# The second half of the input projection by seven products for eight: a decoder trunk on one core

## The chip, the core and the metric

The kernel runs on one core of a Trainium2 chip. A core has a matrix engine (TensorE, PE in the profile; its weight loads are PEld), a vector engine (VectorE, DVE), a scalar engine for functions (ScalarE, ACT), a general engine (GpSimd, POOL) and SyncE (SP), which here only issues transfers. Data lie in device memory (HBM), in SBUF (128 partitions), or in PSUM, where TensorE writes its sums: eight banks of 128 x 512 float32. The metric is the device time of one execution in microseconds (us); the median of several runs is compared.

## The reference

One decoder layer on x of 2048 positions x 1024 channels, float32:

```python
z = rms_norm(x, g1) @ w_in                       # 1024 -> 3584
lru_x, lru_gate, sc_b, sc_c, sc_x = split(z)     # 1024, 1024, 512, 512, 512
lru_x = causal_conv4(lru_x) + bias
y_lru = rg_lru(lru_x) * gelu(lru_gate)           # 16 heads of 64, gates r and i, a scan over positions
y_sc  = sc_b * causal_conv3(sc_c * sc_x)
x = x + concat(y_lru, y_sc) @ w_out              # 1536 -> 1024
h = rms_norm(x, g2)
gate, up = split(causal_conv3(h @ w_up))         # 1024 -> 6144
x = x + (gelu(gate) * up) @ w_down               # 3072 -> 1024
out = rms_norm(x, gf)
```

In the RG-LRU, r and i are sigmoids of 64 x 64 products per head, a = exp(-8 r softplus(-lambda)), and h[t] = a[t] h[t-1] + sqrt(1 - a[t]^2) i[t] x[t].

## The kernel before

Channels lie on the partitions, positions along the free dimension. The positions are worked in two halves of T = 1024, each of two blocks of NB = 512 (a PSUM bank holds 128 channels x 512 positions). Every operand of a product is split into two parts (`split`, L197 to L199: ScalarE makes the rounded part, VectorE the rest), and each product is three matmuls: high x high, high x low, low x high.

The order on TensorE, SyncE and GpSimd is the order in which the program is written (`manual_schedule`). ScalarE and VectorE are ordered by a planner, by priority: earlier in the program comes first, and `high_priority` moves an instruction ahead (HP = 120 for what empties PSUM, HW = 90 for weights of plain products). That order is fixed when the program is built. SyncE issues transfers one after the other; a transfer whose source is not ready holds the ones behind it. `defer(n, ...)` puts a store on a list and `tick()` (called with each load of weights) counts it down and issues what is due.

The stages, in order: input projection of half 0 (`in_phase(0)`), output product of half 0 (`sweeps(0)`), input projection of half 1 (`in_phase(1)`), output product of half 1, up product of half 0, down product of half 0, up and down product of half 1.

The input projection is a plain product: 28 output blocks of 128 channels (`in_product`), each 8 chunks of 128 input channels x 3 x 2 blocks of positions = 48 matmuls, into two banks. The result is multiplied by the inverse root of the mean square while it leaves PSUM (`evac`). Blocks 0 to 7 are lru_x, 8 to 15 lru_gate, 16 to 19 sc_b, 20 to 23 sc_c and 24 to 27 sc_x. They are consumed by units in the order UNITS: L0 to L7 are the LRU blocks (`lru_conv`, `lru_gates`, `lru_scan`), S0 to S3 the gated convolutions (`sc_first`, `sc_second`). Two units together give the operands of the output product (`combine_even`, `combine_odd`), which are stored to device memory (y_d) and read again by the sweeps.

The output, up and down products already use a scheme of seven products of half-size blocks in place of eight (in the manner of Strassen and Winograd): `sweeps` for output and down, with the sums of weights made in device memory by transfers that add (`sums`, `sum_step`), and `Pair` for the up product, with the sums of weights made on VectorE (`up_weights`) and the seven operands B11, B21, B22, T1 to T4 of the other side made by `h_prep`. A Pair makes two output blocks at once with 7 x 4 chunks x 3 = 84 matmuls. One bank collects W11 B11, then S2 T2, S3 T3 and W22 T4, and is copied out after each; two more banks take S1 T1 + S4 B22 and W12 B21, which are added on VectorE.

Pages in SBUF are taken from pools: "act" of 28 pages of 128 x 1024, "w" of 10 (split weights), "tmp" of 7, "wr" of 4 raw pages of 128 x 1536, and four longer pages for what needs a halo. An instruction that needs a page waits until the earlier owner is done with it.

The x of half 1 is prepared beside the output product of half 0 (`x1_beside`, `x_prep`), unnormalised.

## Time and profile before

| what | us |
|---|---|
| runs shown: 2275.12, 2275.98, 2272.85; median | 2275.12 |
| profiled execution, span from first to last instruction | 2273.5 |
| TensorE busy in it | 2254.4 (99%) |
| VectorE busy | 1721.1 (76%) |
| ScalarE busy | 1178.9 (52%) |
| GpSimd busy | 138.2 (6%) |
| input projection of half 0, from 5.7 | 323.6 |
| output product of half 0, from 329.3 | 114.2 |
| input projection of half 1, from 443.5 | 325.3 |
| output product of half 1, from 768.8 | 116.4 |

Of the profiled execution the span is the time that its trace gives; the time beside it, the median, is that of other executions, timed without a trace. The stages are read from the chain of waits, where TensorE changes from one product's tile to the next (zin_b: input projection; ox and oy: output; zx, za, zc: up; dx and dy: down). A matmul's duration in the profile overlaps that of its neighbours, so a count of matmuls is turned into time by the distance of their starts. "Idle before, <- releaser" names what an instruction waited for.

### The profile page before, as it was taken

How to read it: one execution, taken by the hardware profiler on the slowest of the kernel's cores; microseconds unless marked ns; L12 is line 12 of the kernel's file. 1: busy time of each engine (PE TensorE's matmuls, PEld its weight loads, DVE VectorE, ACT ScalarE, POOL GpSimd, SP SyncE). 2: the span in 40 equal slices, each digit the busy share in tenths (PEclk: the TensorE clock that was granted, in tenths of full speed). 3: DMA queues.
4: the chain of work that ended last, by engine and by line, in shares of the span. 5: the costliest groups of instructions: out<-in, count | busy, mean ns of one | idle time of the engine just before them, and what ended most of it. 6: DMA issues, size and time to landing. Idle time of an engine off the chain costs nothing.

```text
span 2273.5 us, 26241 instructions
## 1 busy us (share of the span) xinstructions
PE 2254.4 (99%) x9982; PEld 1855.7 (82%) x9982; DVE 1721.1 (76%) x1956; ACT 1178.9 (52%) x1311; POOL 138.2 (6%) x188
## 2 busy tenths in 40 slices
PE   9999999999999999999999999999999999999997
PEld 7888888888887888888888888888888888888886
DVE  8765678758757898888888887587888888886556
ACT  6674745564668255544444444454544444443343
POOL 0100000010000000111111100000100000000000
PEclk9999999999999999999999999999999999999999
DMA  8642258768644586233232357676223232358755
GB/s 275 141 139 74 70 175 297 274 166 217 195 123 136 199 282 204 92 107 107 98 111 95 113 190 263 207 250 201 70 105 114 92 117 88 118 183 319 259 194 176
DMA packets 146446, 377.24 MB, mean 166 GB/s; under 512 B 14160, under 2 KB 17872, under 8 KB 145744
## 3 DMA queue, kind: packets, MB, share of 16 engines
q1 hardware_dynamic: 136384, 356.69, 45.5%
q0 software_dynamic: 9792, 18.88, 5.1%
q8 instruction: 78, 1.28, 0.2%
q14 instruction: 48, 0.39, 0.0%
q10 hardware_dynamic: 144, 0.00, 0.0%
HBM read 288.48 MB, written 124.78 MB: 182 GB/s over the span
## 4 chain that ended last, share of the span: by engine, by line
PE 91%; ACT 4%; DVE 3%; issue 1%; DMA 0%; DVEq 0%; SPq 0%; ACTq 0%
PE zx L632 23%; PE zin_b L241 20%; PE dx L752 11%; PE zc L632 11%; PE dy L752 9%; PE za L632 6%; PE ox L752 6%; PE oy L752 4%; DVE cv L302 1%; ACT r L343 1%; ACT i L343 1%; PE zr_b L333 0%; ACT L343 0%; DVE r L356 0%; DVE wl_in L199 0%
## 5 line engine op out<-in xcount | busy, mean ns | idle before, releaser
L241 PE MATMUL zin_b<-xh,wh_in 128*128 128x512 f32 x896 | 280.2, 394 | 3.8 <-ACT i L343 3.3
L241 PE MATMUL zin_b<-xl,wh_in 128*128 128x512 f32 x896 | 277.1, 390 | 0.0
L241 PE MATMUL zin_b<-xh,wl_in 128*128 128x512 f32 x896 | 276.8, 390 | 0.0
L241 PEld LDWEIGHTS zin_b<-xh,wh_in 128*128 128x128 f32 x896 | 167.8, 189 | 45.2 <-ACT i L343 4.4
L241 PEld LDWEIGHTS zin_b<-xl,wh_in 128*128 128x128 f32 x896 | 169.1, 189 | 35.5 <-DVE xl L418 0.3
L241 PEld LDWEIGHTS zin_b<-xh,wl_in 128*128 128x128 f32 x896 | 168.8, 188 | 35.3
L199 DVE TENSOR_TENSOR fl_d<-wrf_d,fh_d 128x1024 fp32r<-128x1024 f32 x84 | 102.8, 1223 | 120.9 <-ACT fh_d L198 118.5
L198 ACT ACTIVATE fh_d<-wrf_d 128x1024 fp32r<-128x1024 f32 x84 | 89.0, 1060 | 202.5 <-PE dy L752 83.4
L199 DVE TENSOR_TENSOR wla_up<-wra_up,wha_up 128x1024 fp32r<-128x1024 f32 x48 | 58.8, 1226 | 141.6 <-ACT wha_up L198 141.6
L752 PE MATMUL dx<-fh_d,wh_d 128*128 128x512 f32 x384 | 149.4, 389 | 0.0
L752 PE MATMUL dx<-fl_d,wh_d 128*128 128x512 f32 x384 | 149.4, 389 | 0.0
L752 PE MATMUL dx<-fh_d,wl_d 128*128 128x512 f32 x384 | 149.4, 389 | 0.0
L632 PE MATMUL zc<-hhB,whd_up 128*128 128x512 f32 x384 | 126.0, 389 | 0.0
L302 DVE SCALAR_TENSOR_TENSOR cu<-un,prm,cu 128x1024 f32<-128x1024 f32 x96 | 122.6, 1277 | 4.3 <-ACT cu L298 4.3
L302 DVE SCALAR_TENSOR_TENSOR cg<-ug,prm,cg 128x1024 f32<-128x1024 f32 x96 | 122.8, 1279 | 0.4
L643 ACT ACTIVATE ug<-zx 128x512 f32<-128x512 f32 x96 | 57.6, 600 | 126.1 <-PE zx L632 126.1
L632 PE MATMUL zx<-ht,whc_up 128*128 128x512 f32 x384 | 118.2, 389 | 0.0
L752 PE MATMUL dy<-fh_d,wh_d 128*128 128x512 f32 x288 | 112.0, 389 | 0.0
L752 PE MATMUL dy<-fl_d,wh_d 128*128 128x512 f32 x288 | 112.0, 389 | 0.0
L752 PE MATMUL dy<-fh_d,wl_d 128*128 128x512 f32 x288 | 112.0, 389 | 0.0
L199 DVE TENSOR_TENSOR wl_d<-wrw_d,wh_d 128x1024 fp32r<-128x1024 f32 x84 | 102.4, 1219 | 12.3 <-ACT wh_d L198 10.9
L199 DVE TENSOR_TENSOR wl_in<-wr_in,wh_in 128x1024 fp32r<-128x1024 f32 x53 | 64.6, 1219 | 58.1 <-ACT wh_in L198 58.1
(267 smaller groups left out, 5576.1 us busy)
## 6 DMA issues: line engine op xcount, KB each, us to landing
wr_in<-in_w_in SPq DMA_DIRECT2D x53, 512.0 KB, 5.7
wra_up<-in_w_up SPq DMA_DIRECT2D x48, 512.0 KB, 4.6
wrb_up<-in_w_up SPq DMA_DIRECT2D x48, 512.0 KB, 5.1
f_d_T<-cg SPq DMA_DIRECT2D x96, 256.0 KB, 2.5
wrw_d<-sd_d_S SPq DMA_DIRECT2D x48, 512.0 KB, 4.6
wrf_d<-f_d_T SPq DMA_DIRECT2D x48, 512.0 KB, 3.9
f_d_B<-cu SPq DMA_DIRECT2D x72, 256.0 KB, 2.4
wrw_d<-in_w_down SPq DMA_DIRECT2D x36, 512.0 KB, 4.7
```

Source lines behind the costliest of these rows:

```text
L198: nc.scalar.activation(r32(hi), src, AF.Copy)
L199: nc.vector.tensor_tensor(r32(lo), src, hi, ALU.subtract)
L241: nc.tensor.matmul(ps[t], r32(a), r32(b[:, blk(t)]), start=(first and i == 0), stop=(last and i == 2))
L302: nc.vector.scalar_tensor_tensor(dst, src[:, k : k + T], col(o_w + k), dst, ALU.mult, ALU.add)
L343: nc.scalar.activation(dst[rows, blk(b)], p[HALVES[at], :], AF.Sigmoid, bias=col(o + c)[rows, :])
L632: nc.tensor.matmul(ps, r32(p[:, s]), r32(self.hs[k][x][o]), start=f and i == 0, stop=l and i == 2, skip_group_check=True,)
L643: nc.scalar.activation(dst, self.x, AF.Copy)
L752: nc.tensor.matmul(ps[m], r32(p), r32(x[:, k, :]), start=first and i == 0 and n == 0, stop=(last or not on_x) and i == ni - 1 and n == 2, ...
```

## The change

The second half's input projection now uses the scheme of seven products too.

- The first half, which loads and splits every block of w_in anyway, adds two blocks' halves on VectorE in place (`pair_sums`, three additions of 128 x 512 for each pair of blocks) and stores the sums (si_d). It also stores the split gate weights (sg_d).
- The order of units becomes L0 L1 S0 S1 L2 to L7 S2 S3, with the two gated convolutions of a pair done together.
- Beside the first half's units the x of half 1 is read, squared and summed, its mean taken, and the first of four groups of operands made (`beside_first`, `x1_prep`, which shares `operands` with `h_prep`; the norm is now applied before the products). The other three follow beside the sweeps of half 0, at steps 3, 8 and 14.
- The second half runs `in_blocks`: 14 pairs in the order PAIRS, L for lru_x and lru_gate, X for sc_c and sc_x, B for two blocks of sc_b. Each pair's seven weights are split into seven pages (`in_weights`). An LRU block's gates and scan are worked during the next pair. Its r and i take pages of "tmp", the stored gate weights of four blocks are loaded into a "tmp" page at the first block of the four.
- The first pair of this stage and of each up product runs chunk by chunk: seven banks at once, each chunk of input channels through all seven products (`spread`).
- The inverse norm of half 0's output is stored (ms_d) and read back in the next sweeps. The four preparations of the up product of half 0 all move beside the sweeps of half 1 (steps 1, 6, 11, 16; before, one in the projection, and three at steps 3, 8, 14).
- The pool "w" of ten is cut into "w" and "v" of five each, which plain products use in turn.

```diff
-UNITS = [(u[0], int(u[1])) for u in "L0 L1 S0 L2 L3 S1 L4 L5 L6 L7 S2 S3".split()]
+UNITS = [(u[0], int(u[1])) for u in "L0 L1 S0 S1 L2 L3 L4 L5 L6 L7 S2 S3".split()]
+PAIRS = [(u[0], int(u[1])) for u in "L0 L1 X0 X1 B0 L2 L3 L4 L5 L6 X2 L7 X3 B2".split()]
...
+BLOCKS = {
+    **{("L", c): (c, 8 + c) for c in range(8)},
+    **{("X", g): (20 + g, 24 + g) for g in range(4)},
+    **{("B", g): (16 + g, 17 + g) for g in range(0, 4, 2)},
+}
+PAIR_OF = {o: (PAIRS.index(p), i) for p, ab in BLOCKS.items() for i, o in enumerate(ab)}
+
+TERMS = [("W11", "B11"), ("S2", "T2"), ("S3", "T3"), ("W22", "T4"), ("S1", "T1"), ("S4", "B22"), ("W12", "B21")]
...
+        return page(name, "wv"[turn[0] % 2], 5)
...
+    def load_weights(o, name, gate=None):
         tick()
+        raw_of[o] = raw_tile(f"wr_{name}")
+        out = next(load_parts(w_in[o], name, 1, gate, raw_of[o]))
+        i, _ = PAIR_OF[o]
+        pair_sums(*BLOCKS[PAIRS[i]])
         return out
+
+    def pair_sums(a, b):
+        if a not in raw_of or b not in raw_of:
+            return
+        i, _ = PAIR_OF[a]
+        ra, rb = raw_of.pop(a), raw_of.pop(b)
+        with tc.high_priority(offset=HW):
+            for t, k, x, y in (
+                (rb, 2, rb[:, 0, :], rb[:, 1, :]),
+                (rb, 0, rb[:, 0, :], ra[:, 0, :]),
+                (ra, 0, ra[:, 0, :], rb[:, 2, :]),
+            ):
+                nc.vector.tensor_tensor(t[:, k, :], x, y, ALU.add)
+        defer(2, si_d[i][:, 0:2, :], rb[:, 0:3:2, :])
+        defer(2, si_d[i][:, 2, :], ra[:, 0, :])
...
+        defer(1, sg_d[c // 4, :, c % 4, :], gw[:, : 2 * P])
...
+        r, i = (flat((home or act)(f"{x}{n}")) for x in "ri")
+        a = big(f"a{n}", c % 2)[:, :T] if home else flat(act(f"a{n}"))
...
+    def keep_y(half, n, y, when):
+        if n % 2 == 0:
+            yc = flat(tmp(f"yc{half}_{n}"))
+            even_y[n // 2] = (y, yc)
+            combine_even(y_d[half], when[0], n // 2, y, yc)
         else:
-            pss = [in_product(o, half, acts) for o in (0, NLRU)]
+            even, yc = even_y.pop(n // 2)
+            combine_odd(y_d[half], when[1], n // 2, even, y, yc, flat(tmp(f"yd{half}_{n}")))
...
+            keep_y(half, n, y, (2, 8) if n >= NOUT - 2 else (7, 7))
...
+        def spread(self):
+            self.open()
+            ps = {w: pst(f"z{w}{self.name}") for w, _ in TERMS}
+            for k in range(4):
+                for w, x in TERMS:
+                    self.run(ps[w], w, x, True, True, (k,))
+            (g0, g1), (n0, n1) = self.g, self.n
+            self.x = ps["W11"]
+            self.copy(g0)
+            with tc.high_priority(offset=HP):
+                for dst, w, src in (
+                    (g1, "S2", g0),
+                    (n1, "S3", g1),
+                    (n0, "W22", n1),
+                    (n1, "S1", n1),
+                    (g1, "S1", g1),
+                    (g1, "S4", g1),
+                    (g0, "W12", g0),
+                ):
+                    nc.vector.tensor_tensor(dst, ps[w], src, ALU.add)
+            self.second_done()
+            self.first_done()
...
+            if j == 0:
+                cur.spread()
+                nxt.begin()
+                nxt.sum1()
...
+    def in_weights(i):
+        a, b = BLOCKS[PAIRS[i]]
+        one, other = raw_tile(f"wra_in{i}"), raw_tile(f"wrb_in{i}")
+        nc.sync.dma_start(one[:, 0, :], w_in[a][:, :NB])
+        nc.sync.dma_start(one[:, 1:3, :], si_d[i][:, 1:3, :])
+        nc.sync.dma_start(other[:, 0, :], w_in[a][:, NB:])
+        nc.sync.dma_start(other[:, 1, :], w_in[b][:, NB:])
+        nc.sync.dma_start(other[:, 2, :], si_d[i][:, 0, :])
+        tick()
+        out = {}
+
+        def operand(name, src):
+            w = page(f"w{name}_in{i}", "v" if i == 0 and name in ("W22", "S4") else "w", 5)
+            split(w[:, 0, :], w[:, 1, :], src)
+            out[name] = (w[:, 0, :], w[:, 1, :])
+
+        operand("W11", one[:, 0, :])
+        operand("S1", one[:, 1, :])
+        operand("S2", one[:, 2, :])
+        nc.vector.tensor_tensor(one[:, 2, :], one[:, 2, :], other[:, 0, :], ALU.add)
+        operand("W12", other[:, 0, :])
+        operand("S3", other[:, 2, :])
+        operand("W22", other[:, 1, :])
+        operand("S4", one[:, 2, :])
+        return out
...
+        def load_gates(q):
+            t = tmp(f"gp{q}")
+            state["gw"] = flat(t).rearrange("p (c k) -> p c k", c=NLRU // 2)
+            nc.sync.dma_start(state["gw"], sg_d[q])
+
+        def finish(pair):
+            n = UNITS.index(("L" if pair.kind == "L" else "S", pair.unit))
+            if pair.kind == "L":
+                c = pair.unit
+                xc, cv = lru_conv_of(c, half, pair.first, vpage)
+
+                def gated():
+                    if c % 4 == 0:
+                        load_gates(c // 4)
+                    g = state["gw"][:, c % 4, :]
+                    return lru_gates(c, half, xc, (g[:, :P], g[:, P:]))
+
+                def scanned(pss):
+                    y = lru_scan(c, half, cv, pair.other, *pss, home=tmp, sign=-1.0)
+                    keep_y(half, n, y, (1, 1))
+
+                gates[pair.name] = (gated, scanned)
+            elif pair.kind == "X":
+                pr, cc = pair.first[:, 2 : 2 + T], pair.other
+                nc.vector.scalar_tensor_tensor(pr, pr, -1.0, cc, ALU.mult, ALU.mult)
+                cv = flat(vpage(f"sv{pair.name}"))
+                conv(cv, pair.first, 3, O_SCW + 3 * pair.unit)
+                sv[pair.unit] = cv
+            else:
+                for i, b in enumerate((pair.first, pair.other)):
+                    cv = sv.pop(pair.unit + i)
+                    for t in range(T // NB):
+                        h = blk(t)
+                        nc.vector.scalar_tensor_tensor(cv[:, h], cv[:, h], -1.0 if i else 1.0, b[:, h], ALU.mult, ALU.mult)
+                    keep_y(half, n + i, cv, (1, 1))
...
+        cur = InPair(0, hs, wts[0])
+        last = None
+        for j in range(len(PAIRS)):
+            if j + 2 < len(PAIRS):
+                wts.append(in_weights(j + 2))
+            else:
+                tick()
+            nxt = InPair(j + 1, hs, wts[j + 1]) if j + 1 < len(PAIRS) else None
+            if j == 0:
...
+                cur.spread()
+                nxt.begin()
...
+            if last is not None:
+                gated, scanned = gates.pop(last)
+                pss = gated()
+                scanned(pss)
+                last = None
+            if nxt is not None and j + 2 < len(PAIRS):
+                nxt.sum1()
+            if j > 0:
+                cur.end()
+            finish(cur)
+            if cur.name in gates:
+                last = cur.name
+            start(j)
...
+    def beside_first(n):
+        if n == 0:
+            ss1[1] = acc_tile("a1")
+        if 1 <= n <= KC:
+            t = x1_raw.pop(n - 1)
+            if n == 1:
+                nc.scalar.activation(ss1[1], t, AF.Square)
+            else:
+                nc.scalar.activation(t, t, AF.Square)
+                nc.vector.tensor_tensor(ss1[1], ss1[1], t, ALU.add)
+        if n < KC:
+            t = x1_raw[n] = flat(act(f"xs{n}"))
+            nc.sync.dma_start(t, xT[n, :, T:S])
+        if n == KC:
+            x1_raw["mean"] = mean_split(ss1[1], "a1")
+        if n == KC + 1:
+            inv_rms(ss1[1], "a1", x1_raw["mean"])
+        if n == KC + 2:
+            hx.append(x1_prep(0, ss1[1]))
...
+        if s in (3, 8, 14):
+            hx.append(x1_prep(len(hx), ss1[1]))
...
+    def beside_blocks(j):
+        if j == 0:
+            inv_rms(ss2[0], "b0", mean0)
+            defer(1, ms_d, ss2[0])
+        sum_step()
+        sum_step()
+
+    in_blocks(hx, beside_blocks)
...
+    prepare = h_beside(0, (1, 6, 11, 16))
+
+    def out1_beside(s):
+        if s == 0:
+            t = acc_tile("b0r")
+            nc.sync.dma_start(t, ms_d)
+            rs2[0].append(t)
+        prepare(s)
...
```

276 lines of the change are left out of this document (154 added, 122 removed).

## The prediction

> **What bounds the kernel now.** I read first the page, for who is busy; then the chain of waits, for which engine carries the end; then windows over the stages the change touches; then single rows for prices.
>
> ```profile
> span 2273.5 us, 26241 instructions
> PE 2254.4 (99%) x9982; PEld 1855.7 (82%) x9982; DVE 1721.1 (76%) x1956; ACT 1178.9 (52%) x1311; POOL 138.2 (6%) x188
> ...
> L241 PE MATMUL zin_b<-xh,wh_in 128*128 128x512 f32 x896 | 280.2, 394 | 3.8 <-ACT i L343 3.3
> ```
>
> TensorE is busy 2254.4 of 2273.5 us, so what shortens the kernel is fewer matmuls, and what lengthens it is a new gap in front of one. The 394 ns of a row here are not the price of a matmul, since they overlap. The chain of waits (start, length, what) has the price and the borders of the stages:
>
> ```profile
> 54.14 11.10 PE zin_b L241 x48
> ...
> 443.53 21.76 PE zin_b L241 x96
> ...
> 768.83 15.65 PE ox L752 x69
> ...
> 803.59 16.32 PE ox L752 x72
> ```
>
> 96 matmuls took 21.76 us: 0.2267 us each. The second half's input projection runs from 443.53 to 768.83, and the first two sweeps of the output product behind it end at 803.59: 360.1 us for both. The stages' windows (length, then busy us of PE, PEld, DVE, ACT, POOL):
>
> ```profile
> 5.70:329.30 323.60, 322.74 (x1445) 262.20 (x1446) 224.57 (x288) 203.57 (x227) 11.95 (x13) 1.00 0.48 148
> 329.30:443.50 114.20, 114.20 (x505) 94.59 (x505) 97.25 (x108) 62.76 (x63) 0.00 (x0) 1.00 0.73 256
> 443.50:768.80 325.30, 322.81 (x1450) 262.45 (x1449) 217.00 (x233) 195.08 (x210) 21.66 (x25) 0.99 0.63 178
> 768.80:885.20 116.40, 114.88 (x506) 94.51 (x505) 106.16 (x120) 57.03 (x59) 0.34 (x4) 1.00 0.74 253
> ```
>
> In the projection of the second half VectorE works 217 and ScalarE 195 of 325.3 us, two thirds and 60%; in the sweeps behind it VectorE already works 106 of 116.4.
>
> **The gross gain.** 28 products of 48 matmuls (1344) become 14 pairs of 84 (1176). 168 x 0.2267 = 38.1 us. In full, the new stage without any gap is 1176 x 0.2267 = 266.6, eight gate products at 1.66 (the first gate row below, at 52.48, to the projection's row at 54.14) = 13.3, one mean of four matmuls 0.9, and the two sweeps 2 x 16.32 = 32.6: 313.4 us. Against 360.1 that is 46.7 less, so it also wins back 8.6 us that the stage loses now. The mean of the second half's x moves into the first half (0.9 us of PE), which leaves 45.8.
>
> ```profile
> 52.48 0.49 PE L333 MATMUL zr_b<-xch,gw 64*128 64x512 f32 x1
> ...
> 661.05 0.49 PE L333 MATMUL zr_b<-xch,gw 64*128 64x512 f32 x1
> ...
> 684.62 0.49 PE L333 MATMUL zr_b<-xch,gw 64*128 64x512 f32 x1
> ...
> 722.53 0.50 PE L241 MATMUL zin_b<-xh,wh_in 128*128 128x512 f32 x1 [1.58 <-ACT i L343]
> 723.93 0.79 PE L241 MATMUL zin_b<-xh,wh_in 128*128 128x512 f32 x1 [0.90 <-ACT i L343]
> ```
>
> The last two rows are part of those 8.6 us: TensorE waits 1.58 and 0.90 us for sigmoids to empty banks. What follows them (length, busy us, clock):
>
> ```profile
> 722.00:724.00 2.00, 0.57 (x2) 0.84 0.00 0
> 724.00:726.00 2.00, 2.00 (x5) 0.50 0.00 0
> 726.00:728.00 2.00, 2.00 (x9) 0.81 0.81 272
> ```
>
> The granted clock falls to 0.50 and costs 2 x (0.16 + 0.50 + 0.19) = 1.7 us more. I add 1.7 us to each new gap that is longer than this one. The Trainium skill ("TensorE: Matmul & The Clock Gate", Part 1) says that throttling needs an idle window of about 3.4 us; here 2.5 us were enough, and the measurement decides. By the Trainium skill the shortest of the gaps below would go without the surcharge, 1.7 us less in the sum.
>
> **Load on the other engines.** Their prices, VectorE first, then ScalarE:
>
> ```profile
> L199 DVE TENSOR_TENSOR whd_up<-wrb_up,whd_up 128x512 fp32r<-128x512 f32 x48 | 32.9, 685 | 0.0
> L647 DVE TENSOR_TENSOR ug<-zc,ug 128x512 f32<-128x512 f32 x48 | 32.8, 684 | 0.0
> L302 DVE SCALAR_TENSOR_TENSOR cv<-xl,prm,cv 128x1024 f32<-128x1024 f32 x48 | 61.4, 1279 | 2.6 <-ACT cv L300 1.9
> L346 DVE TENSOR_TENSOR i<-i,cv 128x1024 f32<-128x1024 f32 x16 | 19.6, 1223 | 39.6 <-ACT i L343 39.6
> L356 DVE TENSOR_TENSOR_SCAN r<-a,h_last,i 128x1024 f32<-128x1024 f32 x8 | 18.8, 2348 | 0.1
> ```
> ```profile
> L198 ACT ACTIVATE whd_up<-wrb_up 128x512 fp32r<-128x512 f32 x48 | 30.3, 631 | 86.4 <-PE za L632 82.8 <-issue 3.4
> L643 ACT ACTIVATE ug<-zx 128x512 f32<-128x512 f32 x96 | 57.6, 600 | 126.1 <-PE zx L632 126.1
> L343 ACT ACTIVATE r<-zr_b,prm 64x512 f32<-64x512 f32 x32 | 21.9, 684 | 0.6
> L343 ACT ACT_TABLE_LOAD x17 | 21.8, 1283 | 0.3
> L348 ACT ACTIVATE a<-r,nc 128x1024 f32<-128x1024 f32 x16 | 18.4, 1152 | 0.2
> L198 ACT ACTIVATE xch<-cv 128x1024 fp32r<-128x1024 f32 x16 | 17.0, 1061 | 62.9 <-DVE cv L302 62.9
> ```
>
> A pair gives VectorE seven splits, an addition and three additions from PSUM: 11 x 0.685 = 7.5 us; ScalarE seven splits and four copies: 7 x 0.631 + 4 x 0.600 = 6.8. An LRU block adds on VectorE 3 x 1.28 + 5 x 1.22 + 2.35 = 12.3; on ScalarE eight sigmoids 5.5, four table loads 5.1, exp and tanh 2.3, and five passes near 1.06: 18.2. So in a pair behind an LRU block ScalarE needs 25.0 us and VectorE 19.8 plus 1.4 for the combinations of y, where TensorE needs 84 x 0.2267 + 1.66 = 20.7. Over the stage ScalarE comes to 14 x 6.8 + 8 x 18.2 + 7 = 248 and VectorE to 14 x 7.5 + 8 x 12.3 + 41 (gated convolutions, combinations, mean) = 244, of 281. It fits on average, but not in the run L2 to L6.
>
> The Trainium skill ("ScalarE: Activation LUTs", What ACT_TABLE_LOAD costs) puts a switch of tables at 1.28 us of loading and some 1.38 us of draining; that would make ScalarE 248 + 32 x 1.38 = 292 of 281 and the bound. The rows below show the load at 673.56 and the sigmoid 1.29 us behind it, without a drain, so I use 1.28.
>
> **New gap 1: the gates of L4.** The gate weights of L4 to L7 are fetched by load_gates in the SP queue right where they are needed, behind tick's five stores of y of L2 and L3. Those wait for the last combination after the scan of L3, and whatever stands behind them on SP waits too. Rows: ScalarE's chain of L5 and the start of L6, VectorE's end of L5, SP's five stores and the next issue, SP's waits, a load's landing.
>
> ```profile
> 673.56 1.28 ACT L343 ACT_TABLE_LOAD   x1
> 674.85 0.68 ACT L343 ACTIVATE r<-zr_b,prm 64x512 f32<-64x512 f32 x1
> ...
> 702.55 0.68 ACT L343 ACTIVATE r<-zr_b,prm 64x512 f32<-64x512 f32 x1
> ```
> ```profile
> 694.29 2.35 DVE L356 TENSOR_TENSOR_SCAN r<-a,h_last,i 128x1024 f32<-128x1024 f32 x1
> ...
> 702.60 0.68 DVE L530 SCALAR_TENSOR_TENSOR yd<-yc,r 128x512 f32<-128x512 f32 x1
> ```
> ```profile
> 701.58 0.33 SPq L195 DMA_DIRECT2D y_d_T<-yc  x1
> ...
> 704.03 0.65 SPq L366 DMA_DIRECT2D sd_d_S<-in_w_down  x1
> ```
> ```profile
> SPq L195 <- DVE r L360: 213.2, 8, 49.2
> ```
> ```profile
> wrw_o<-in_w_out SPq DMA_DIRECT2D x18, 512.0 KB, 5.5
> wrf_o<-y_d_T SPq DMA_DIRECT2D x24, 512.0 KB, 4.8
> ```
>
> From the gates of L3 to those of L4 TensorE has 20.7 us of work. Meanwhile the chain must run: eight sigmoids 5.5, three table loads 3.8, exp and square 2.2, m, sqrt, i*m 3.5, scan 2.35, y 1.2, three combinations 2.1: 20.7 at least, after 1.66 of gates. Five stores take 704.03 - 701.58 = 2.45, the load 4.8. Lower end: 1.66 + 20.7 + 2.45 + 4.8 = 29.6, a gap of 8.9. Upper end: L5 took from its gates at 661.05 to 703.28, 42.2 us; with stores and load 49.5, a gap of 28.8. SP has already been held 49.2 us by one such y; today weights loaded ahead cover it. I take 10, near the lower end, because a stopped TensorE hands out no other work. With the clock 11.7.
>
> **New gap 2: X2.** Temporary pages are seven. At the second copy of the pair behind an odd LRU block eight are wanted (gate weights, y and difference of the even block, the odd block's output, r and i, and the outputs of two pairs); the copy waits until the scan frees i, and TensorE's fourth product waits for the copy. It is due 18.0 us after the gates of L5. The scan ends 1.66 + 17.4 at best and the copy 0.6 later: 1.7 late; by L5's rows (661.05 to 696.64) 18.2 late. I take 3, with its clock.
>
> **New gap 3: into the sweeps.** The last stores of L7 stand in SP's queue ahead of the first loads of the sweep, and only X3's last product and B2 lie between: 1.66 + 7 x 2.72 = 20.7 us from L7's gates. Chain and gates 22.4, stores 2.45, two copies of weight sums at 0.65, load 5.5, two first splits 2.1: 33.7, a gap of 13; by L5's row 32. Now six products stand there and hide it. I take 13, with the clock 14.7.
>
> **Smaller terms.** At the start of the stage two operand pages come free only with the last matmul of the sweep: 0 to 3, I take 1. In the first half VectorE gets 42 weight sums (28.8), seven additions of squares (8.5), the mean (5) and the first operands (2 x 1.28 + 5 x 0.685 + 3 x 1.22 = 9.6): 224.6 + 52 = 276 of 324, and six LRU blocks now follow one another instead of two and four. They lag already: the sigmoids of L5 and L6 stand 27.7 us apart, their gates 23.6. 0 to 14, I take 3. The spills of sums and gate weights are DMA work under a share of 0.48: nothing; without that cover SP would issue 36 more in line, some 16 us spread over 320. The first sweeps trade eight preparations (18.8 on VectorE) for three of 9.6: 97 + 10 = 107 of 114.2, as full as the second sweeps are now: nothing, or up to 2. The chunkwise pair holds seven of the eight banks; the next pair's first product takes the eighth and runs 2.72 us, in which a copy of 0.60 frees another: nothing. The second sweeps get a fourth preparation, 106 + 9.6 of 116, and the chunkwise first pair of the up product gives the last one 3 x 21 x 0.2267 = 14.3 us of cover: 0 to 5, I take 1.
>
> **Sum.** 2273.5 - 45.8 + 11.7 + 3 + 14.7 + 1 + 3 + 1 = 2262.1 of span. The runs' median, 2275.12, lies 1.6 above the span shown: 2263.7, called 2264.
>
> **Rivals.** (a) SP does not hold the gates and the sweep up: LRU chains end earlier than any row here shows, or loads overtake. Gaps 1 and 3 vanish: 2264 - 26 = 2238. For it: no sustained wait on TensorE in the trace. Against it: the chain alone fills the time. Chance 0.14. (b) The slower side: the LRU chain paces the projection, because r and i lie in seven temporary pages and ScalarE is over its time. Five chains (L2 to L6) at 27.7 instead of 20.7 us are 35 us in place of gaps 1 and 2; with gap 3, 7 in the first half (six at 4.1 less the 17.9 by which L6's sigmoids lag its gates now) and 2 small: 58.7, so 2273.5 - 45.8 + 58.7 + 1.6 = 2288. It makes the kernel slower from a period of 20.7 + (45.8 - 23.7)/5 = 25.1 us. For it: ScalarE's 25.0 and the 27.7; against it: part of the 27.7 is work that a waiting TensorE does not send. Chance 0.22. (c) The same gaps halfway to their upper ends in one place, 11 us more: 2275, no change. Chance 0.14.
>
> **How the numbers follow.** My own case has 0.50: 2264. Below it stands (a), above it (b) and (c). About 0.2% is what a measurement of this kernel tells from no change, 2270.6 to 2279.7. Faster: 0.14 + 0.50 = 0.64; the same 0.14; slower 0.22. The range leaves out half of (a) below and half of (b) above, and is 2238 to 2288; my own case alone spans 2250 to 2270.
>
> **What would show it.** Right: 168 matmuls fewer; a stage of about 300 us; a gap of some 10 us ahead of one gate product two thirds through it, its releaser a DMA of gate weights; a gap of some 13 us at the first matmul of the second output sweeps, with SP waiting for VectorE before it; half a clock after each. Wrong: TensorE without gaps there (a); many gaps of 3 to 8 us with ScalarE as releaser at every LRU pair (b); a gap at the start of the up product, which would mean that the fourth preparation is late.

## The result: 12% slower, and the profile after

| | before | after |
|---|---|---|
| runs, median (lowest to highest), us | 2273.98 (2272.53 to 2275.98) | 2546.36 (2543.66 to 2548.74) |
| profiled execution's span, us | 2273.5 | 2545.9 |
| input projection of half 0, us | 323.4 | 518.0 |
| output product of half 0 | 114.2 | 116.2 |
| input projection of half 1 | 325.3 | 375.5 |
| output product of half 1 | 116.4 | 138.0 |
| up product of half 0 | 457.9 | 461.3 |

The ratio is 1.1196, with a 95% interval from 1.1180 to 1.1211. The forecast was 2264, its range 2238 to 2288. A stage is counted here, and for every kernel below, from its first product to the first product of the next stage, so that a wait ahead of a stage counts to the one before it. The five differences make 194.6 + 2.0 + 50.2 + 21.6 + 3.4 = 271.8 of the span's 272.4 us.

The head of the page of the kernel after, and its windows over these five stages (length, then busy us of PE, PEld, DVE, ACT, POOL, then granted clock, share of the DMA engines, GB/s):

```profile
span 2545.9 us, 26290 instructions
PE 2275.8 (89%) x9814; PEld 1854.2 (73%) x9814; DVE 1812.3 (71%) x2108; ACT 1233.6 (48%) x1427; POOL 136.2 (5%) x187
```
```profile
5.67:523.62 517.95, 349.53 (x1449) 277.01 (x1449) 276.38 (x352) 219.22 (x243) 11.39 (x13) 0.82 0.38 116
523.62:639.78 116.16, 114.54 (x506) 94.52 (x504) 106.82 (x125) 57.74 (x62) 0.00 (x0) 1.00 0.88 304
639.78:1015.29 375.51, 304.97 (x1278) 240.26 (x1276) 235.36 (x290) 235.89 (x309) 21.43 (x24) 0.92 0.55 154
1015.29:1153.33 138.04, 125.88 (x504) 100.69 (x505) 113.33 (x128) 63.32 (x65) 0.20 (x2) 0.92 0.75 265
1153.33:1614.60 461.27, 458.44 (x2021) 378.97 (x2020) 377.94 (x438) 228.49 (x270) 61.73 (x93) 1.00 0.32 108
```

The 168 matmuls are gone (9982 to 9814). But TensorE stands still in two stages where it had been busy throughout. The largest loss is not in the stage that was rewritten. It is in the first half, whose matmuls did not change.

**The first half.** Its waits, SyncE's first and then TensorE's (us in total, times, longest):

```profile
SPq L1039 <- PE zr_b L373: 111.1, 3, 43.0
SPq L608 <- DVE sv L338: 77.0, 1, 77.0
SPq L211 <- DVE wr_in L265: 71.0, 8, 25.3
SPq L1039 <- PE zi_b L373: 39.9, 1, 39.9
```
```profile
PE zin_b L277 <- ACT wh_in L214: 145.9, 9, 21.8
```

L1039 is the load of one chunk of half 1's x into a page of the pool "act"; L608 is the load of the first operands; L211 is the store of whatever `tick` finds due (`tick` issues the stores that were put off). One turn of what follows from it, on TensorE, SyncE and ScalarE in the kernel after:

```profile
264.05 0.49 PE L373 MATMUL zr_b<-xch,gw 64*128 64x512 f32 x1
...
287.48 1.22 PE L277 MATMUL zin_b<-xh,wh_in 128*128 128x512 f32 x2 [21.77 <-ACT wh_in L214]
335.63 1.22 PE L277 MATMUL zin_b<-xh,wh_in 128*128 128x512 f32 x2 [21.82 <-ACT wh_in L214]
```
```profile
265.77 0.33 SPq L1039 DMA_DIRECT2D xs<-in_xT  x1
...
270.08 3.27 SPq L237 DMA_DIRECT2D wr_in<-in_w_in  x2
```
```profile
285.42 1.06 ACT L393 ACTIVATE cv<-cv 128x1024 f32<-128x1024 f32 x1 [0.18 <-DVE cv L392]
286.38 1.99 ACT L214 ACTIVATE wh_in<-wr_in 128x1024 fp32r<-128x1024 f32 x2
```

The x load's page comes free only with the gates' products, at 264 to 265.7 us. SyncE has stood at it, and the stores and the next two blocks' weights stand behind it. They go out at 270, when TensorE has already run dry. They land within 5.3 us of their issue, by about 278. On ScalarE their rounding then stands, in its fixed order, behind the whole LRU chain that the same gates released, and ends at 288. So TensorE waits 21.8 us, and the next turn repeats that 48 us later. The first part of such a wait is the hold on SyncE, the second the place of the rounding in ScalarE's order. The page that SyncE waits for is freed by TensorE, and TensorE waits for what SyncE holds.

**The second half.** TensorE's waits in the projection and into the sweeps:

```profile
735.53 5.07 PE L673 MATMUL zxin<-htx,wW_in 128*128 128x512 f32 x12 [6.50 <-ACT soin L684]
...
856.89 5.49 PE L673 MATMUL zxin<-htx,wW_in 128*128 128x512 f32 x12 [7.48 <-ACT soin L684]
866.31 0.76 PE L373 MATMUL zr_b<-xch,gp 64*128 64x512 f32 x1 [3.93 <-DMA gp<-sg_d]
...
956.57 3.01 PE L673 MATMUL zxin<-htx,wW_in 128*128 128x512 f32 x12 [2.15 <-ACT soin L684]
...
1015.29 0.80 PE L967 MATMUL ox<-fh_o,wh_o 128*128 128x512 f32 x1 [5.16 <-ACT fh_o L214]
```

The rows of one kind are summed in its waits: for each of the eight scans there is one wait of TensorE for the copy of a pair's bank (soin).

```profile
PE zxin L673 <- ACT soin L684: 51.2, 8, 10.0
```

At 856.24 that copy had waited for the scan to give its page free; five of the eight copies, or one just ahead of them on ScalarE, waited so for a page, 23.2 us in all:

```profile
856.24 0.60 ACT L684 ACTIVATE soin<-zxin 128x512 f32<-128x512 f32 x1 [4.08 <-DVE r L397]
```

Behind such a wait the 12 matmuls can run at a slower clock. The eight rows take 3.01 to 5.49 us. The shortest, at 956.57, ran at full clock (granted clock 1.00 from 957 to 959). Against it the other seven are 1.4 to 2.5 us longer, and the mean of all eight is 1.6 us longer.

### The profile page after: what moved, and what is told of

Same layout as the page of the kernel before. It is cut to its first block, busy times and chain, and to the rows that moved or that the text cites. A ratio compares the mean times of both kernels' runs of the same rounds, so it can differ in the third digit from the quotient of the medians.

```text
span 2545.9 us, 26290 instructions
## 1 busy us (share of the span) xinstructions
PE 2275.8 (89%) x9814; PEld 1854.2 (73%) x9814; DVE 1812.3 (71%) x2108; ACT 1233.6 (48%) x1427; POOL 136.2 (5%) x187
## 4 chain that ended last, share of the span: by engine, by line
PE 76%; DVE 10%; ACT 8%; issue 3%; DMA 2%; SPq 0%; DVEq 0%; ACTq 0%
PE zx L673 20%; PE zin_b L277 11%; PE zc L673 10%; PE dx L967 10%; PE dy L967 8%; PE za L673 5%; PE ox L967 4%; PE zxin L673 4%; PE oy L967 2%; DVE cv L338 2%; ACT r L384 1%; ACT i L384 1%; PE zcin L673 1%; PE zS L673 1%; DVE r L397 1%
## 5 line engine op out<-in xcount | busy, mean ns | idle before, releaser
L277 PE MATMUL zin_b<-xh,wh_in 128*128 128x512 f32 x448 | 148.8, 415 | 145.9 <-ACT wh_in L214 145.9
L277 PEld LDWEIGHTS zin_b<-xh,wh_in 128*128 128x128 f32 x448 | 89.6, 202 | 169.2 <-ACT wh_in L214 149.7
L277 PE MATMUL zin_b<-xh,wl_in 128*128 128x512 f32 x448 | 146.2, 409 | 11.6 <-DVE wl_in L215 11.6
L277 PE MATMUL zin_b<-xl,wh_in 128*128 128x512 f32 x448 | 146.1, 408 | 0.2
L673 PE MATMUL zc<-hhB,whd_up 128*128 128x512 f32 x368 | 120.7, 389 | 0.0
L277 PEld LDWEIGHTS zin_b<-xh,wl_in 128*128 128x128 f32 x448 | 88.1, 198 | 34.1 <-DVE wl_in L215 15.6
L684 ACT ACTIVATE ug<-zx 128x512 f32<-128x512 f32 x92 | 55.0, 598 | 114.8 <-PE zx L673 114.7
L277 PEld LDWEIGHTS zin_b<-xl,wh_in 128*128 128x128 f32 x448 | 89.2, 200 | 21.0 <-DVE xl L460 1.4
L214 ACT ACTIVATE wh_d<-wrw_d 128x1024 fp32r<-128x1024 f32 x84 | 88.0, 1048 | 22.2 <-DMA wrw_d<-sd_d_S 7.4
```

Source lines behind the costliest of these rows:

```text
L214: nc.scalar.activation(r32(hi), src, AF.Copy)
L277: nc.tensor.matmul(ps[t], r32(a), r32(b[:, blk(t)]), start=(first and i == 0), stop=(last and i == 2))
L673: nc.tensor.matmul(ps, r32(p[:, s]), r32(self.hs[k][x][o]), start=f and i == 0, stop=l and i == 2, skip_group_check=True,)
L684: nc.scalar.activation(dst, self.x, AF.Copy)
```

## The experiments

Stage times come from a profiled execution of each kernel; the run times beside them are of the same kernel, with 2273 to 2276 for the kernel before beside it. The kernels before, after, e16 and e18 were timed four times or more, the others once. Line numbers in rows are those of each kernel, and the edits are shown shortened. The expectations of e3 (150.5 us for the second sweeps) and e4 (369 for the projection) set the border between these two stages elsewhere than the table (138.0 and 375.5).

| kernel | time, us | half 0 projection | sweeps 0 | half 1 projection | sweeps 1 |
|---|---|---|---|---|---|
| before | 2273.98 | 323.4 | 114.2 | 325.3 | 116.4 |
| after | 2546.36 | 518.0 | 116.2 | 375.5 | 138.0 |
| e1_no_x | 2421.7 | 374.0 | 132.6 | 378.5 | 136.4 |
| e2_queue | 2434.7 | 393.7 | 128.9 | 377.0 | 133.4 |
| e3_late | 2547.9 | 517.0 | 116.2 | 375.8 | 137.2 |
| e4_merged | 2549.7 | 518.9 | 116.2 | 377.2 | 135.6 |
| e5_spillq | 2463.0 | 426.5 | 125.4 | 377.8 | 134.2 |
| e6_vsplit | 2545.5 | 518.3 | 116.2 | 374.2 | 135.4 |
| e7_spill_nox | 2402.7 | 356.3 | 133.1 | 377.8 | 133.7 |
| e8_pages | 2530.7 | 518.7 | 116.2 | 361.5 | 134.8 |
| e9_pages_vsplit | 2532.3 | 518.7 | 116.2 | 364.2 | 131.8 |
| e10_no_sums | 2401.0 | 363.6 | 131.0 | 376.1 | 131.2 |
| e11_gates | 2391.9 | 354.3 | 126.5 | 377.0 | 133.2 |
| e12_no_lru | 2458.0 | 518.3 | 116.2 | 283.7 | 137.1 |
| e13_mean | 2381.2 | 337.9 | 132.3 | 375.3 | 135.3 |
| e14_order | 2544.9 | 516.9 | 116.2 | 356.2 | 153.1 |
| e15_preps | 2546.6 | 518.4 | 116.2 | 378.1 | 134.8 |
| e16_best | 2371.1 | 340.6 | 135.0 | 361.9 | 134.1 |
| e17_stores | 2544.4 | 517.6 | 116.2 | 374.0 | 135.9 |
| e18_all | 2368.1 | 338.0 | 132.0 | 361.2 | 134.1 |

### The first half: what holds SyncE

**Without the second half's x (e1), and with its loads on another queue (e2).**

```diff
 e1
     def beside_first(n):            # load, square, add, mean, x1_prep(0)
...
+        pass
-        if s in (3, 8, 14):
-            hx.append(x1_prep(len(hx), ss1[1]))
+        if s in (1, 6, 11, 16):
+            hx.append(x1_prep(len(hx), ss1[0]))
 e2
+        return operands(..., rs, nc.sync if k else nc.gpsimd)
-            nc.sync.dma_start(t, src(kk))
+            queue.dma_start(t, src(kk))
-            nc.sync.dma_start(t, xT[n, :, T:S])
+            nc.gpsimd.dma_start(t, xT[n, :, T:S])
```

> Left out of the changed kernel: the first half no longer loads, squares and averages the second half's x (the second half is scaled with the first half's mean square, so its values are another's), and all four preparations of the second half's operands stand in the first sweeps. The weight sums and their spills stay. SyncE theory (x loads whose page is not free hold the weight loads behind them on SyncE's queue): the first-half projection falls from 518 us to 325-345, the execution from 2546 to 2353-2373, and VectorE's sums and spills together cost at most some 20 us. Rival (the sums, the two parities of weight pages, or the raw pages that wait for a partner and for their spills are what is slow): the first half stays above 450 us, the execution above 2475.

> One thing is changed: the eight x loads of the first half and the two loads of the first preparation are issued by GpSimd instead of SyncE, in the same places of the program, into the same pages. The whole computation stays. SyncE theory: their waits now hold only GpSimd's queue, so the first-half projection falls from 518 us to 330-360 and the execution to 2358-2388, though the loads wait for their pages just as long. Rival (it is the pages themselves, or the squares and adds of the second half's x on ScalarE and VectorE): the first half stays above 450 us, the execution above 2475.

In the program e2 changes nothing but the queue of ten loads, and it takes 124 us from the first half: 518 to 394. (The execution gains 112, since the first sweeps grow by 13.) So what these loads cost on SyncE is shown. How it splits is not. The planner gave ScalarE another order as well: in e2 four roundings of w_in's blocks stand ahead of the first sigmoids (38.27 to 59.16, sigmoids from 65.05), in the kernel after one (38.44; sigmoids from 59.12). And at three of TensorE's large waits in the kernel after, 43.7 us of the 145.9, the weights had been there in time. Those of the product at 74.87, which waited 20.1 us, were issued at 43.97, landed 4.9 us later, and were rounded only at 73.78. No run keeps ScalarE's order and changes the queue alone.

Both theories missed the size: e1 and e2 end at 374 and 394, above the range and far under the rival's 450. Something else was still holding SyncE. Its wait in e1, with the issues around it, and TensorE's two large waits there:

```profile
SPq L211 <- DVE gw L215: 117.4, 7, 38.2
```
```profile
154.33 2.12 SPq L211 DMA_DIRECT2D si_d<-wr_in  x2
194.71 0.32 SPq L211 DMA_DIRECT2D sg_d<-gw  x1
195.09 0.91 SPq L237 DMA_DIRECT2D wr_in<-in_w_in  x2
```
```profile
206.31 1.22 PE L277 MATMUL zin_b<-xh,wh_in 128*128 128x512 f32 x2 [18.18 <-ACT wh_in L214]
275.32 1.22 PE L277 MATMUL zin_b<-xh,wh_in 128*128 128x512 f32 x2 [18.92 <-ACT wh_in L214]
```

sg_d is the spill of the split gate weights, due one tick after the split is written in the program. From 156.5 to 194.7 SyncE waits for that split, and the next block's weights leave right behind it. Every split gate block adds such a store.

**The spills on GpSimd, with the x loads there (e5) and without them (e7).**

```diff
-        defer(2, si_d[i][:, 0:2, :], rb[:, 0:3:2, :])
+        defer(2, si_d[i][:, 0:2, :], rb[:, 0:3:2, :], nc.gpsimd)
 (so too the third sum and sg_d; e5 on top of e2, e7 on top of e1)
```

> As e2_queue, and the spills of the weight sums and of the split gate weights are issued by GpSimd too; the whole computation stays. In e2_queue the first-half projection takes 394 us, 70 more than before the change, and in e1_no_x, where no x load is left, 374. Spill theory (a spill that waits for VectorE's sum or split stands on SyncE's queue ahead of the next units' weight loads and holds them; two waits of TensorE for ScalarE's rounded weights, of 17 and 21 us, come from it): the first half falls to 325-350 us, the execution from 2435 to 2366-2391. Rival (VectorE's sums themselves, or raw pages held for the partner block and the spill): the first half stays at 375-400 us, the execution above 2410.

> As e1_no_x (no work for the second half's x in the first half, so the second half is scaled by another mean; all four preparations in the first sweeps), and the spills are issued by GpSimd, whose queue holds nothing else there but the accumulations of the output weights' sums. In e5_spillq the spills stood behind x loads on GpSimd and the raw weight pages were late. Spill theory (what e1_no_x still lost, 374 us against 323, is spills on SyncE's queue ahead of weight loads): the first half falls to 325-345 us, the execution from 2422 to 2373-2393. Rival (the sums and the raw pages held for a partner and a spill cost it on any queue): the first half stays at 365-385 us, the execution above 2410.

Neither came out as the spill theory had it, nor quite as the rival. e5 is worse than e2, 426 us, since the spills now stand behind x loads whose page is not free:

```profile
SPq L237 <- DMA si_d<-wr_in: 253.9, 10, 53.4
```

A raw weight page is free only once its sums are stored, so a late spill holds the next weight load just as a late x load did. e7 takes 18 us from e1's first half (374.0 to 356.3). Both waits of 18 us are gone, and TensorE waits 1.4 us in all for rounded weights; its largest waits are for ScalarE's sigmoids and for the split of the convolution's result (xch), 4.5 to 5.3 us each. SyncE's wait is still there, 187.7 us in all behind the gate spills on GpSimd, but without the x loads the weights come in time. Moving a hold to another queue thus helped where nothing that was needed soon stood behind it there, and cost where something did.

**The sums left out (e10), and the gate spills taken away (e11).**

```diff
 e10 (on e1): pair_sums returns at once; in_weights loads columns of w_in instead of si_d
 e11 (on e2)
-        defer(1, sg_d[c // 4, :, c % 4, :], gw[:, : 2 * P])
...
+            raw = flat(vpage(f"gr{c}"))[:, :P]
+            nc.sync.dma_start(raw, w_gate[c])
+                split(g[:, :P], g[:, P : 2 * P], raw)
```

> As e1_no_x, and the weight sums and their spills are left out of the first half; the second half loads plain weight columns of the same size in their place (other values). The spills of the split gate weights stay on SyncE. Sums theory (raw weight pages held for the partner block, and spills that wait for the sums, are what e1_no_x still loses, 374 us against 323): the first half falls to 323-340 us, the execution from 2422 to 2371-2390. Rival (the gate weights' spills, one tick late on SyncE ahead of the next loads and waiting up to 38 us for VectorE's split, are enough): the first half stays at 355-375 us.

> As e2_queue, and the split gate weights are not spilled at all: the second half loads and splits the gate weights again, one for each pair of LRU blocks, a step ahead of their products. The whole computation stays. Gate-spill theory (e10_no_sums, without the sums and theirs spills, still had both waits of 18 us and 364 us; there SyncE's stores of the split gate weights waited 166 us in all for VectorE's split, ahead of the next weight loads): the first half falls from e2_queue's 394 us to 340-362, the wait for the gates of the fifth LRU block goes from the second half, and the execution falls from 2435 to 2372-2398. Rival (raw pages held for a partner, and the x loads' pages, cost the 70 us that e2_queue still has over before): the first half stays above 378 us.

e10 took the sums and their spills out of e1 and won only 10 us (374 to 364): both waits of 18 us stay, with SyncE's wait for gw the longest of its waits.

```profile
SPq L211 <- DVE gw L215: 166.2, 7, 52.3
```
```profile
197.55 1.22 PE L276 MATMUL zin_b<-xh,wh_in 128*128 128x512 f32 x2 [18.20 <-ACT wh_in L214]
264.88 1.22 PE L276 MATMUL zin_b<-xh,wh_in 128*128 128x512 f32 x2 [18.26 <-ACT wh_in L214]
```

e11 keeps the sums and has no gate spills, and lands where the gate-spill theory said: 354 us from 394, 2391.9. The gates' second splitting costs nothing that shows, and the wait for the gates of the fifth block is gone. One large wait is left:

```profile
302.65 1.22 PE L308 MATMUL ms_a<-rh_a,ones_r 128*128 128x512 f32 x2 [16.41 <-ACT rh_a L213]
```

**The mean of half 1's x taken later (e13).**

```diff
-        if n == KC:          x1_raw["mean"] = mean_split(...)
+        if n == KC + 2:
-        if n == KC + 1:      inv_rms(...)
+        if n == KC + 3:
-        if n == KC + 2:      hx.append(x1_prep(0, ss1[1]))
-        if s in (3, 8, 14):
+        if s in (1, 6, 11, 16):
```

> As e11_gates, and the mean of the second half's x is taken two units later, and all four preparations of its operands stand in the first sweeps. The whole computation stays. Theory (of the 31 us that e11_gates' first half still has over before, 16 are one wait of TensorE's queue for ScalarE's rounded sum of squares, which waits for the last x load): the first half falls from 354 us to 330-342, the first sweeps grow from 126 us to 128-134 by the fourth preparation, the execution falls from 2392 to 2374-2388. Rival (the wait only moves behind): the first half stays at 348-356 us.

As expected: 337.9 us, with the wait gone, and the sweeps 6 us longer for the fourth preparation. So the 195 us of the first half are 124 for x loads on SyncE, 39 for gate spills on it, 16 for the mean that TensorE waits for together with the first preparation, which moved out, and 15 left. These are the steps in the one order in which the things were taken away (e2, e11, e13); in another order the shares can differ. The 15 are in e13's own trace 8.2 of waits, the largest 5.4 for ScalarE's sigmoids, and 7.1 of slower clock, less 0.8 that the kernel before waited. What part of them the sums have no run shows: e10's 10 us are of a kernel without the x work.

### The second half: what a scan holds

**One page less (e4), and the rounding on VectorE (e6).** r is worked in a's page; then the split of the convolution's result moves, and the copies get a higher priority.

```diff
 e4
+            r = a = big(f"a{n}", c % 2)[:, :T]
+            i, q = flat(home(f"i{n}")), flat(spare(f"q{n}"))
 e6 (on e4)
+            nc.vector.tensor_scalar(r32(xc[0]), cv, 1.0, None, ALU.mult)
+            with tc.high_priority(offset=400): nc.scalar.activation(dst, self.x, AF.Copy)
```

> One thing is changed: in the second half's LRU scan the recurrence gate r lives in the halo page of the decay a (tanh is taken ahead of the exponential, which then overwrites r), and the square and the state go to one of the five other weight pages, so that a scan holds one page less of the seven that the copies of the next pair, the scan and the sums for the stores share. The whole computation stays. Page theory (the copies out of PSUM wait for a page that the last scan still holds): the nine waits of 2 to 10 us at the LRU pairs, 51 us in all, fall to under 20, and the second-half projection goes from 369 us to 320-340, the execution to 2497-2517. Rival (ScalarE and VectorE need that long for an LRU pair, whatever page they write): the stage stays above 358 us and the execution above 2535.

> As e4_merged, and in the second-half projection the rounding of the convolution's result is done by VectorE instead of ScalarE, and the planner lifts the copies out of PSUM further ahead, so that neither the page of a scan nor that rounding (ScalarE waited at it for VectorE's last tap) stands before a copy. The whole computation stays. Order theory (each copy waits for whatever ends with VectorE's chain of taps and scan; taking both away lets it go as soon as TensorE is done): the waits at the LRU pairs fall from 51 us to under 20, the stage between the first sweeps and the second from 377 to 320-345 us, the execution from 2550 to 2490-2518. Rival (an LRU pair takes ScalarE and VectorE so long in any order, some 35 us where TensorE needs 21): the stage stays above 365 us.

The stage stays at 377 and 374 us. That looks like the rivals. But the rows show that neither edit cleared the way. In e4 the copy no longer waits for a page; it stands behind the rounding (xch) that waits for VectorE, and goes at the same point as in the kernel after (856.86 for 856.24, in a stage that began 1 us later):

```profile
855.90 1.06 ACT L214 ACTIVATE xch<-cv 128x1024 fp32r<-128x1024 f32 x1 [2.80 <-DVE cv L338]
856.86 0.58 ACT L691 ACTIVATE soin<-zxin 128x512 f32<-128x512 f32 x1
```

In e6 a copy ahead of it waits for the halo page that the scan holds:

```profile
893.24 0.60 ACT L871 ACTIVATE prin<-zxin 128x512 f32<-128x512 f32 x1 [5.60 <-DVE q L408]
893.74 0.59 ACT L871 ACTIVATE soin<-zxin 128x512 f32<-128x512 f32 x1
```

**The scan's pages apart (e8), and the rounding moved as well (e9).** Without the fourth preparation seven pages are free for r, i and a.

```diff
-        if s in (3, 8, 14):
+        if s in (3, 8):
+    hx.append(hx[2])
-                    y = lru_scan(..., home=tmp, sign=-1.0)
+                    y = lru_scan(..., home=act, sign=-1.0)
```

> Left out of the changed kernel: the fourth preparation of the second half's operands; the products take the third's operands in its place (other values, the same instructions). The seven pages that it held are free, and the LRU scan of the second half puts r, i and a there, so that it takes nothing of the pages that the copies of the next pair use. Page theory: the waits of the copies at the LRU pairs go, 51 us to under 20, and the second-half projection, 376 us from its first product to the first of the sweeps, falls to 310-340 us, the execution from 2546 to 2470-2512. Rival (the LRU's chain through ScalarE and VectorE takes some 36 us a pair, where the products need 21, whatever pages there are): the stage stays above 360 us, the execution above 2530.

> As e8_pages (the fourth preparation left out, the scan's pages apart), and as in e6_vsplit VectorE rounds the convolution's result and the planner lifts the copies. In e8_pages all eight waits that were left at the LRU pairs, 27 us, stood behind ScalarE's rounding of the convolution's result, which waited for VectorE's last tap. Two-covers theory (page and rounding each hold the same copy until VectorE's chain is through, so that taking either alone shows little): the copies' waits at the LRU pairs fall under 12 us, the stage from 361 to 318-342 us, the execution to 2485-2510. Rival (VectorE and ScalarE are the limit in any order, with 235 us of work each and both in a chain): the stage stays above 352 us.

e8 halves the copies' waits and wins 14 us of the stage, a partial answer between the two theories. That is about what the page waits come to: the copies' waits shrink by 24.3 us (51.2 to 26.9) where pages had cost 23.2. Of the eight copies that are still late five stand behind the rounding, and not all eight, as e9's expectation says; the other three stand behind the square root and a weight's rounding. e9 takes the rounding away too and wins nothing more, so the two-covers theory fell: the next thing in ScalarE's order stands before the copy, now a table load and the square root. The rows are e8's sum of waits, then of e9 the bank's last matmul, at 845.39, and what ScalarE did until the copy at 849.21.

```profile
PE zxin L673 <- ACT soin L684: 26.9, 8, 4.7
```
```profile
845.39 0.39 PE L677 MATMUL zxin<-hhB11x,wW_in 128*128 128x512 f32 x1
```
```profile
846.95 1.28 ACT L397 ACT_TABLE_LOAD   x1
848.25 1.06 ACT L397 ACTIVATE cv<-cv 128x1024 f32<-128x1024 f32 x1
849.21 0.58 ACT L864 ACTIVATE soin<-zxin 128x512 f32<-128x512 f32 x1
```

**No scan at all (e12).**

```diff
-                    y = lru_scan(c, half, cv, pair.other, *pss, home=tmp, sign=-1.0)
-                    keep_y(half, n, y, (1, 1))
+                    keep_y(half, n, pair.other, (1, 1))
```

> Left out of the changed kernel: in the second half the LRU's sigmoids, decay, scan and gelu; the gates' products stay, and the second block of a pair is stored as the unit's output. LRU theory (all that the second-half projection loses against its products comes from copies that wait, in ScalarE's and VectorE's order or for a page, behind an LRU scan): the waits at the pairs fall under 12 us, TensorE's clock stays near full, and the stage falls from 376 us to 285-315. Rival (the copies' own round trips, the loads of the spilled sums, or the splits of eight weight operands a pair limit it): the stage stays above 335 us.

```profile
640.17:923.91 283.74, 282.62 (x1277) 229.25 (x1276) 178.25 (x246) 113.09 (x173) 21.43 (x24) 1.00 0.72 202
```

283.7 us, TensorE busy in all but 1.1 of them, at full clock. So the seven products alone do bring what was counted, 325.3 - 283.7 = 41.6 us. The eight scans cost 375.5 - 283.7 = 91.8, 11.5 us each, which is 69.4 of waiting and 22.4 of slower clock (PE busy 305.0 against 282.6). e12 takes the scans' work away together with their pages and their places in the order, so it shows what the scans cost; that the places are the larger part is argued from e8, e9 and the rows.

**Other orders of the pairs (e14, e16).**

```diff
 e14  "L0 X0 L1 X1 L2 B0 L3 L4 X2 L5 X3 L6 L7 B2"     (on the kernel after)
 e16  "L0 L1 X0 L2 X1 L3 B0 L4 L5 X2 L6 L7 X3 B2"     (on e13)
```

> One thing is changed: the order of the 14 pairs of the second half, so that other pairs stand between LRU pairs (L0 X0 L1 X1 L2 B0 L3 L4 X2 L5 X3 L6 L7 B2). The whole computation stays. Pace theory (an LRU pair takes ScalarE and VectorE about 36 us where the products need 21, and two in a row make the second wait; other pairs between them give the time back): the stage falls from 376 us to 325-355 and the execution to 2495-2530. Rival (each scan holds the next pair's copies, whatever the next pair is: with no LRU the stage took 284, so the eight scans cost 11.5 us each): the stage stays at 368-384 us.

> As e13_mean, with another order of the pairs (L0 L1 X0 L2 X1 L3 B0 L4 L5 X2 L6 L7 X3 B2), in which no more than two LRU pairs follow each other and the last LRU pair is not next to the sweeps. The whole computation stays. Pace theory: the waits at the LRU pairs shrink where another pair follows, and since X3 and B2 stand between the last scan and the sweeps nothing moves into these: the second half's projection and sweeps together, 375 + 135 us in e13_mean, fall by 15 to 30 us, the execution from 2381 to 2350-2367, still 3 to 4% slower than before. Hold theory (a scan holds the next pair's copies, whatever pair that is): they fall by less than 8 us, the execution stays above 2373.

e14 moved 19 us out of the stage and 15 into the sweeps, since the last scan (L7's) now stands in them. Those 15 lie in one wait of 20.37 us at the second step, whose loads left SyncE only at 1016.1, behind the stores of that scan and of B2 (1008.2 to 1014.8). e16 won 14.6 us over projection and sweeps together against e13 (510.6 to 496.0) and 10 of the execution, which lies between what the pace and the hold theory gave. Its waits speak for the hold: still one for each scan, and nearly as long in all as in e13 (46.2). So these waits don't account for the 14.6 us, and what does is open.

```profile
PE zxin L671 <- ACT soin L682: 44.2, 8, 9.6
```

### The second sweeps

**Later stores (e3), later preparations (e15), both and more (e17).**

```diff
 e3   keep_y(..., (1, 3 if n == 9 else 1));  (2, 3) for the last B
 e15  h_beside(0, (3, 8, 13, 18))
 e17  e15 and keep_y(..., (1, 6 if n == 9 else 1));  (1, 5) for the last B
```

> One thing is changed: the stores of the last two units of the second-half projection are issued one or two ticks later, so that fewer stand ahead of the first loads of the sweeps behind. Gap theory (as the prediction had it): what is lost at the start of those sweeps, some 10 us of TensorE's waits between 1007 and 1030 us, goes, the sweeps fall from 150.5 us to 140-144, the execution to 2536-2540. Rival (VectorE, with four preparations of the up products' operands in these sweeps, is what makes them long, and only moves its waits): the sweeps stay at 148-152 us, the execution within 3 us of 2546.

> One thing is changed: the four preparations of the up products' operands in the second sweeps stand at steps 3, 8, 13 and 18 instead of 1, 6, 11 and 16, so that the first two operands are loaded after the first three steps' loads. Theory (the sweeps' slow start, TensorE idle 15 us in their first 42, is the preparation's loads and VectorE's work ahead of the next steps' loads and splits): the sweeps fall from 138 us to 122-130, the execution to 2532-2540. Rival (the first loads come 7 us ahead of the sweeps where they came 19 us ahead before, because the last units' results and stores come late): the sweeps stay at 135-140 us.

> The changed kernel with the last stores of the second-half projection further back: those of its last two odd units go out five or six ticks later, behind the first five steps' loads of the sweeps, and the preparations stand at steps 3, 8, 13 and 18, so that for the first three steps only two early stores stand among the loads on SyncE. The whole computation stays. Queue theory (the sweeps' slow start is loads that stand on SyncE behind stores that wait for the last units' results; in e3_late these stores only moved from before the first loads to between the first and the second): the sweeps fall from 138 us to 118-128, the execution to 2528-2537. Rival (splits of the sweeps' operands come late in VectorE's order, behind the last units' work): the sweeps stay at 133-140 us.

None of them moved it: 137, 135 and 136 us against 138, and e12, with no scan before it, has 137. SyncE's issues at the start, of the kernel after, with the first and the second step's loads and a store between them:

```profile
1007.77 0.58 SPq L980 DMA_DIRECT2D wrw_o<-in_w_out  x1
...
1012.33 3.85 SPq L211 DMA_DIRECT2D y_d_T<-yc  x2
...
1019.03 0.59 SPq L980 DMA_DIRECT2D wrw_o<-in_w_out  x1
```

And of e17, where the first step's loads leave at 968.96 and two stores are left between them and the second step's:

```profile
1006.76 0.32 SPq L211 DMA_DIRECT2D y_d_B<-svin  x1
1016.23 0.32 SPq L211 DMA_DIRECT2D y_d_T<-yc  x1
...
1017.07 0.44 SPq L980 DMA_DIRECT2D wrw_o<-in_w_out  x1
```

The second step's loads leave at 1019.0 and at 1017.1, 3 to 4 us after the first product of the sweeps (1015.3 and 1013.9), because a store that waits for the last pair's difference (yc) stands ahead of them. In the kernel before they went out 41 us ahead of the first product at 768.7 (the 19 us in e15's expectation are those of the third step's):

```profile
727.57 0.37 SPq L765 DMA_DIRECT2D wrw_o<-in_w_out  x1
```

This fits the hold that the prediction saw there, and e14's wait of 20.37 us fits it too. For the first step's loads it is shown: in the kernel after they left behind L7's five stores (1005.27 to 1007.16) and TensorE waited 5.16 us for them, and in e3 and e17, which put those stores later, the first product waits for nothing. But the projection is not shorter for it (375.8 and 374.0 us): the last pair waits longer for its copy there (9.42 us against 7.87) and goes on at 1006.4 and 1006.9, where it had gone on at 1002.8. And in e17 a wait of 5.16 us stands at the second step instead. For the second step no kernel with the loads ahead of every such store was run, so there it stays argued.

### All that helped, together (e18)

```diff
 e18 = e16 + e17's stores and preparations
```

> All that helped and keeps the whole computation together: x loads on GpSimd, no spill of the gate weights, mean two units later, preparations in the sweeps, the order of pairs of e16_best, and the stores and preparations of e17_stores. If the queue theory of e17_stores holds: 10 to 18 us under e16_best's 2371, 2353 to 2361, 3.4 to 3.8% over before. If not, 2366 to 2376.

2368.1 us (2364.4 to 2375.8), a ratio of 1.0422 with an interval from 1.0400 to 1.0444; e16 has 1.0420 (1.0403 to 1.0438). The two cannot be told apart, so the queue theory's 10 to 18 us are not there. Two thirds of the loss are undone, 178 of 272 us, and the kernel before stays the faster one.

## Why the prediction was wrong, point by point

- **Gross gain: right.** 168 matmuls fewer, and without the scans 41.6 us less in the stage (e12), where 38.1 were counted.
- **The first half, "0 to 14, I take 3", and the spills, "nothing": the step that failed.** The stage measured 194.6 us more. The step counted VectorE's additions and called the spills DMA work under a share of 0.48. It did count issues, 36 more in line for some 16 us, as the price without cover, but an issue is not what a queue costs. What it did not ask is what each new entry on SyncE's queue waits for. The eight x loads and the first operands' loads were not priced at all, though gap 1 in the same text is this mechanism. Behind them stood weights that TensorE needs (e2: 124 us, with the change of ScalarE's order that came with it; e11: 39). VectorE's part was sized well: 276 us of work were forecast, and 276.4 are in the first window. The sums and their spills cost some 10 us in a kernel without the x work (e10), inside the range.
- **Gap 1, gates of L4: right in place and cause**, 3.9 us instead of 10, since the wait for a copy of 7.5 us stands just before it and had let the gates' load catch up. Where that copy's wait was shorter, in e8, the gap was 8.9.
- **Gap 2, a copy waiting for the scan's page: the right mechanism, told of one place.** "At the second copy of the pair behind an odd LRU block" it was 3 us once; it is one wait for each of the eight scans, 51.2 us, and with free pages half of it stays behind other work of ScalarE (e8, e9).
- **Rival (b) was nearer for the second half.** Its mark, gaps at every LRU pair with ScalarE as releaser, is what the trace shows. Its price, 35 us for five chains, was too small: 91.8 for eight (e12). The work was forecast well (ScalarE 248, VectorE 244; measured 235.9 and 235.4). What failed is the reading of a sum of work under the stage's length as room. The work comes in one in-order chain, and TensorE's next product hangs on one copy in it. How the 91.8 us split between order, pages and work is not shown beyond e8's 14.
- **Gap 3, 13 us at the first product of the second sweeps: right in place and cause, too large.** It measured 5.16 us (at 1015.29, counted in the projection), and SyncE stood at L7's stores before it; in e3 and e17 this wait is gone, and other waits take its place.
- **The second sweeps themselves, "0 to 5, I take 1": 21.6 us.** They are 10.6 of waits and 11.0 of slower clock (PE busy 125.9 against 114.8). The forecast asked what VectorE has to do there, and not what the second step's loads wait for; they stand behind B2's stores. The rest of the size is not explained.
- **Half a clock after a gap, 1.7 us: about the right size, for too few gaps.** The mean of the eight rows above is 1.6 us, from 0 to 2.5. It was added for two gaps; the projection of half 1 lost 22.4 us to the slower clock (e12), and the first half ran at a mean clock of 0.82.
- **The first sweeps, 0 to 2: 2.0 measured, in part by luck.** It holds in the kernel after, whose first half had run late. In every kernel with a faster first half these sweeps take 125.4 to 135.0 us, 11 to 21 more than before.

## What to carry to other kernels

Price a transfer that is added to an in-order queue by what it waits for and by who needs what stands behind it, not by its bytes or its issue time; ask above all whether the page or the result it waits for is freed by the engine that needs the loads behind it, since then the wait feeds itself. An engine's sum of work under a stage's length is not room: a product that needs a copy between its steps waits for whatever stands ahead of that copy in the copier's order, and taking away one such thing uncovers the next. When a large block of the loss sits in a stage whose matmuls did not change, look at the queues first, with one kernel that changes only the queue, and see whether a planner has changed another engine's order along with it.
